# Shifting three layouts of on-chip memory by a few hundred bytes

## The chip, the cores and the metric

The kernel runs on one NeuronCore of a Trainium2 chip, as one program. The metric is the device time of one execution in microseconds. TensorE (PE in the profile) does the matrix products out of SBUF, the on-chip memory of 128 partitions, into PSUM; VectorE (DVE), ScalarE (ACT) and GpSimd (POOL) do the element-wise work; DMA queues bring the weights in.

## The reference

One decoder layer on 512 tokens of width 1024, in float32:

```python
h = h + 0.5 * swiglu(rmsnorm(h, ffn1_norm), ffn1_w_gate, ffn1_w_up, ffn1_w_down)   # width 2816
proj = rmsnorm(h, mix_norm) @ w_in                     # 1024 -> u, v, z, xbc, dt
ya = rmsnorm(chunked_spatial_gating(gelu(u), gelu(v), ...), gm_out_norm)
yb = mamba2_mixer(z, xbc, dt, ...)                     # chunked state-space scan
h = h + concat([ya, yb]) @ w_out
h = h + 0.5 * swiglu(rmsnorm(h, ffn2_norm), ffn2_w_gate, ffn2_w_up, ffn2_w_down)
gate = sigmoid(rmsnorm(h, ple_norm) @ ple_w_gate + ple_b_gate)
h = h + gate * (p @ ple_w_proj)
return rmsnorm(h, final_norm)
```

## The kernel before

**Products.** Each float32 operand is split into a rounded part and a remainder (`hi` and `lo`, type float32r), and each product of 128x128 weights with a tile of activations is three matmuls: hi·hi, hi·lo, lo·hi (`passes`). In a matmul one operand is loaded into the array first (a weight load, 128 columns, 512 bytes of each partition), and the other streams through it (256 or 512 columns, 1024 or 2048 bytes of each partition). The weight load of the next matmul runs while the present one streams. The two feed-forward networks use a Strassen-like scheme with seven products, on half the tokens each, so their matmuls have 256 columns (tiles `xfa` and `xfb` stream against `whi` and `wlo`); their first group of columns is done in the plain way with 512 columns.

**Order.** All operations are recorded once, and then issued in a fixed list of steps (`ORDER`). The change leaves this list as it is. Semaphores are worked out from which instruction touches which bytes.

**Memory.** SBUF is laid out in three parts. The base part (`sb`: `tmp`, `h`, `raw`, `whi`, `wlo` and small tiles) stays for the whole kernel and ends at byte 90,976 of each partition. Above it stands a left layout, and down from byte 229,344 a right layout; both are exchanged as the kernel goes on: `ffn1_left`, `mix_left`, `ffn2_left`, `ple_left`, and `ffn1_right`, `mix_right`, `ffn2_right`, `ple_right`. `REGION` (line 55) says which tile is on which side. When a layout is opened (`open_now`, line 342) or closed (`close_now`, line 350), `pad` (line 331) adds an empty tile of `PAD[...]` bytes (line 61). On the left it stands in front of the tiles and moves them up; on the right it stands above them and moves them down. A new layout's tile waits for the users of the old tiles whose bytes it takes.

All large tiles of one layout have sizes that are multiples of 1024 bytes (2060 for `convin` apart), so all of them begin at the same remainder by 512. The weights within a tile are read in pieces of 512 bytes, so a tile's remainder is that of every piece. The remainders by 512, with `whi` and `wlo` of the base part at 384:

| tiles, layout | first byte before | remainder | first byte after | remainder |
|---|---|---|---|---|
| `whi`, `wlo` (base) | 54,144 and 66,432 | 384 | the same | 384 |
| `xfa`, `xfb` (ffn left) | 91,072 and 107,456 | 448 | 91,456 and 107,840 | 320 |
| `x` (mix left, ple left) | 91,136 | 0 | 91,520 | 384 |
| `ghi`, `glo`, `whix`, `wlox` (ffn right) | 163,808 to 225,248 | 480 | 163,712 to 225,152 | 384 |
| `ya`, `yb` (mix right) | 163,712 and 196,480 | 384 | the same | 384 |

What streams against what, and the distance of the streamed operand's first byte from that of the weights being loaded, by 512:

| streamed, loaded | where | distance before | after |
|---|---|---|---|
| `xfa`/`xfb`, `whi`/`wlo` | up and gate products of both networks | 64 | 448 (that is -64) |
| `x`, `whi`/`wlo` | input projections, final gate | 128 | 0 |
| `whi`/`wlo`, `x` | projection of v | 384 | 0 |
| `ghi`/`glo`, `whix`/`wlox` | down products | 0 | 0 |
| `ghi`/`glo`, `whi`/`wlo` | the other down products, per-layer embedding | 96 | 0 |
| `ya`/`yb`, `whi`/`wlo` | output projection | 0 | 0 |

The printed names in the profile are in the order out<-streamed,loaded. Since a recorder issues every operation, all of them have one line, 1943, and groups are told apart by tiles.

Of the kernel before, what the change touches and what calls it, by code (L numbers as in the profile page):

```python
# [57 lines left out]

PAD = {"sb": 0, "ffn_left": 96, "mix_left": 160, "ple_left": 160, "ffn_right": 0, "mix_right": 96, "ple_right": 0}
HEADS = 16
HD = 64
GROUPS = 2
# [218 lines left out]
def layer_kernel(ctx: ExitStack, tc: tile.TileContext, a: dict, out: bass.AP):  # L283
# [47 lines left out]
    def pad(pool, name):  # L331
        n = PAD[name.replace("1", "").replace("2", "")]
        if n:
            pool.tile([P, n // 4], F32, tag="pad", name=name_of("pad"))
# [1717 lines left out]
```

## Time and profile before

| | |
|---|---|
| three runs before | 1113.59, 1114.28 (median), 1115.97 us |
| the profiled execution's own time | 1115.11 us |
| its span from the first to the last instruction | 1113.4 us |
| mean granted TensorE clock | 0.993 |
| busy: PE, weight loads, DVE, ACT, POOL | 1099.0, 967.6, 765.0, 520.2, 127.5 us |

The span is 1.7 us shorter than the execution's time; the rest lies around the instructions. A matmul's recorded duration is longer than its turn, because the next one begins to stream before it has drained: the turn of a matmul is read as the time from its start to the next one's start in the timeline, which merges neighbours of one kind into one row (x2 means two).

### The profile page before, as it was taken

What the parts mean: (1) busy time and instruction counts of PE and PEld (TensorE: products, weight loads), DVE (VectorE), ACT (ScalarE), POOL (GpSimd) and SP (SyncE); (2) the same over time, 40 slices, a digit from 0 to 9 for tenths busy, and PEclk for the clock granted to TensorE, in tenths of its full rate; (3) what the DMA queues carried; (4) which work ended last, traced back from release to release, by engine and by line L of the source; (5) the groups of instructions that cost most, each with busy time, mean ns of one, the idle gap of its engine ahead of it and who ended that gap; (6) DMA issues with size and microseconds to landing.
All of it is one profiled execution on the core that took longest, in us unless ns stands there. A gap on an engine that the chain in (4) does not pass through costs nothing.

```text
span 1113.4 us, 16384 instructions
## 1 busy us (share of the span) xinstructions
PE 1099.0 (99%) x6631; PEld 967.6 (87%) x6631; DVE 765.0 (69%) x1072; ACT 520.2 (47%) x715; POOL 127.5 (11%) x124
## 2 busy tenths in 40 slices
PE   8999999999999999999999999999999999999996
PEld 6899999999998777778877878899999999999886
DVE  6977666666667468766649876687765666766656
ACT  7544443434435336866424444455434433434445
POOL 1100010000000200123103000101100000000212
PEclk9999999999999999999999999999999999999997
DMA  9788468564631224542314133767837674643412
GB/s 318 207 213 245 109 202 229 146 190 133 152 95 57 82 90 153 160 136 79 114 62 133 38 106 122 208 184 179 217 93 204 169 204 139 166 103 123 133 38 76
DMA packets 49036, 161.66 MB, mean 145 GB/s; under 512 B 5568, under 2 KB 5824, under 8 KB 48960
## 3 DMA queue, kind: packets, MB, share of 16 engines
q1 hardware_dynamic: 34128, 117.46, 31.3%
q0 software_dynamic: 9232, 33.56, 16.3%
q10 hardware_dynamic: 5600, 9.60, 2.9%
q8 instruction: 52, 0.85, 0.3%
q14 instruction: 24, 0.20, 0.1%
HBM read 156.33 MB, written 4.26 MB: 144 GB/s over the span
## 4 chain that ended last, share of the span: by engine, by line
PE 92%; DVE 5%; DMA 1%; ACT 1%; issue 1%; POOL 0%; ACTq 0%; SPq 0%; POOLq 0%
PE b L1943 92%; DVE tmp L1943 1%; DVE wlo L1943 1%; DVE xs L1943 1%; DMA g<-in_p 1%; DVE u L1943 0%; DVE x L1943 0%; DVE h L1943 0%; POOL ssum L1943 0%; DVE ya L1943 0%; DMA cs_dram<-csrow 0%; DVE yb L1943 0%; ACT tmp L1943 0%; DVE convin L1943 0%; ACT whi L1943 0%
## 5 line engine op out<-in xcount | busy, mean ns | idle before, releaser
L1943 PE MATMUL b<-xfb,whi 128*128 128x256 f32 (+1 forms) x1664 | 305.8, 284 | 0.0
L1943 PEld LDWEIGHTS b<-xfb,whi 128*128 128x128 f32 x1664 | 259.2, 188 | 7.0 <-issue 1.0
L1943 PE MATMUL b<-xfb,wlo 128*128 128x256 f32 (+1 forms) x832 | 236.3, 284 | 0.0
L1943 DVE TENSOR_TENSOR wlo<-raw,whi 128x1024 fp32r<-128x1024 f32 (+1 forms) x139 | 173.8, 1254 | 66.3 <-ACT whi L1943 66.3
L1943 ACT CAST whi<-raw 128x1024 fp32r<-128x1024 f32 (+1 forms) x140 | 145.1, 1040 | 147.5 <-PE b L1943 107.4
L1943 PE MATMUL b<-x,whi 128*128 128x512 f32 (+1 forms) x640 | 189.3, 382 | 0.7 <-ACT x L1943 0.4
L1943 PEld LDWEIGHTS b<-xfb,wlo 128*128 128x128 f32 x832 | 156.2, 188 | 1.4
L1943 PEld LDWEIGHTS b<-x,whi 128*128 128x128 f32 x640 | 116.1, 188 | 26.5 <-issue 1.5
L1943 PE MATMUL b<-xfa,whi 128*128 128x256 f32 (+1 forms) x704 | 134.4, 289 | 0.0
L1943 PE MATMUL b<-x,wlo 128*128 128x512 f32 (+1 forms) x312 | 117.9, 378 | 0.3 <-DVE wlo L1943 0.3
L1943 PE MATMUL b<-ghi,whix 128*128 128x512 f32 x296 | 116.6, 394 | 0.0
L1943 PE MATMUL b<-ghi,wlox 128*128 128x512 f32 x296 | 116.5, 394 | 0.0
L1943 PE MATMUL b<-glo,whix 128*128 128x512 f32 x296 | 115.3, 390 | 0.0
L1943 PEld LDWEIGHTS b<-xfa,whi 128*128 128x128 f32 x704 | 110.8, 188 | 3.9
L1943 PE MATMUL b<-xfa,wlo 128*128 128x256 f32 (+1 forms) x352 | 102.0, 290 | 0.0
L1943 ACT CAST whi<-rawb 128x1024 fp32r<-128x1024 f32 x52 | 54.5, 1048 | 79.7 <-PE b L1943 56.0
L1943 DVE TENSOR_TENSOR wlo<-rawb,whi 128x1024 fp32r<-128x1024 f32 x52 | 63.3, 1221 | 40.8 <-ACT whi L1943 40.7
L1943 DVE SCALAR_TENSOR_TENSOR h<-b,h 128x512 f32<-128x512 f32 x96 | 64.3, 685 | 29.3 <-PE b L1943 28.9
L1943 ACT CAST whix<-rawd 128x1024 fp32r<-128x1024 f32 (+1 forms) x40 | 39.4, 986 | 84.1 <-PE b L1943 73.2
L1943 PEld LDWEIGHTS b<-x,wlo 128*128 128x128 f32 x312 | 58.7, 188 | 12.6 <-DVE wlo L1943 1.0
L1943 PEld LDWEIGHTS b<-xfa,wlo 128*128 128x128 f32 x352 | 66.1, 188 | 1.4
L1943 DVE TENSOR_TENSOR wlox<-rawd,whix 128x1024 fp32r<-128x1024 f32 (+1 forms) x40 | 45.6, 1140 | 31.1 <-ACT whix L1943 31.1
(229 smaller groups left out, 1644.0 us busy)
## 6 DMA issues: line engine op xcount, KB each, us to landing
raw<-in_ffn_gu SPq DMA_DIRECT2D x56, 512.0 KB, 5.6
rawd<-in_ffn_down SPq DMA_DIRECT2D x40, 512.0 KB, 4.5
rawb<-in_ffn_gu SPq DMA_DIRECT2D x32, 512.0 KB, 5.7
raw<-in_ffn_gu POOLq DMA_DIRECT2D x30, 512.0 KB, 7.6
raw<-in_w_in SPq DMA_DIRECT2D x29, 512.0 KB, 3.7
s<-in_ffn_gu SPq DMA_DIRECT2D x20, 512.0 KB, 5.5
s<-in_ffn_gu POOLq DMA_DIRECT2D x20, 512.0 KB, 7.7
raw<-in_w_out SPq DMA_DIRECT2D x16, 512.0 KB, 3.7
```

What stands on the lines that cost most here:

```text
L1943: getattr(getattr(real, engine), what)(*(real_of(x) for x in args), **{k: real_of(x) for k, x in kw.items()})
```

## The change

The padding of every left layout grows by 384 bytes. On the right, the two layouts that had no padding get 96 bytes, which the mixing layout has already. Nothing else is changed: the operations, their engines, their order and their shapes are the same.

```diff
-PAD = {"sb": 0, "ffn_left": 96, "mix_left": 160, "ple_left": 160, "ffn_right": 0, "mix_right": 96, "ple_right": 0}
+PAD = {"sb": 0, "ffn_left": 480, "mix_left": 544, "ple_left": 544, "ffn_right": 96, "mix_right": 96, "ple_right": 96}
```

All layouts still fit: the highest left tile ends at byte 159,104 (`mix_left`), and the lowest right tile begins at 159,552 (`mix_right`).

## The prediction

> **What bounds the kernel now.** I read the page's busy times first, then the chain of work that ended last, then TensorE's waits, then the timeline of TensorE in stretches without interruption.
>
> ```profile
> span 1113.4 us, 16384 instructions
> PE 1099.0 (99%) x6631; PEld 967.6 (87%) x6631; DVE 765.0 (69%) x1072; ACT 520.2 (47%) x715; POOL 127.5 (11%) x124
> PE 92%; DVE 5%; DMA 1%; ACT 1%; issue 1%; POOL 0%; ACTq 0%; SPq 0%; POOLq 0%
> ...
> PE b L1943 <- DVE tmp L1943: 3.2, 3, 1.7
> ...
> PE b L1943 <- DVE ya L1943: 0.3, 1, 0.3
> PE b L1943 <- DVE x L1943: 0.3, 1, 0.3
> ```
>
> PE is busy 99% of the span, the chain is PE for 92%, and the longest wait of PE on another engine adds up to 3.2 us. The time is therefore the sum of the matmuls' turns. The change alters no instruction, so it can act in two ways: through the turn of a matmul, if that depends on where its operands lie, or through waits, since it shifts which old bytes a new tile takes.
>
> Whether a turn depends on addresses is asked of the timeline. In each pair below, the first and last row are matmuls of the same kind in a stretch of threes (hi·hi, hi·lo, lo·hi); the first column is the start. First `x` against `whi`/`wlo` (distance 128 by 512), then `yb` against them (distance 0):
>
> ```profile
> 405.62 0.40 PE L1943 MATMUL b<-x,wlo 128*128 128x512 f32 x1
> 405.85 0.63 PE L1943 MATMUL b<-x,whi 128*128 128x512 f32 x2
> ...
> 409.12 0.39 PE L1943 MATMUL b<-x,wlo 128*128 128x512 f32 x1
> ...
> 626.97 0.39 PE L1943 MATMUL b<-yb,wlo 128*128 128x512 f32 x1
> 627.20 0.62 PE L1943 MATMUL b<-yb,whi 128*128 128x512 f32 x2
> ...
> 629.69 0.39 PE L1943 MATMUL b<-yb,wlo 128*128 128x512 f32 x1
> ```
>
> Five threes of `x` take 3.50 us, 233.3 ns a matmul; four of `yb` take 2.72 us, 226.7 ns. Shape, weight tiles and granted clock are the same:
>
> ```profile
> 405.50:412.50 7.00, 7.00 (x32) 5.63 (x31) 6.83 (x12) 2.63 (x4) 0.00 (x0) 1.00 0.27 75
> 626.00:633.00 7.00, 7.00 (x32) 5.79 (x32) 4.63 (x7) 5.16 (x8) 0.00 (x0) 1.00 0.26 75
> ```
>
> Columns: PE, PEld, DVE, ACT, POOL, clock, DMA share, GB/s. The clock is 1.00 and DMA alike in both; DVE is busier in one, ACT in the other. What differs is where the streamed tile lies. Further distances:
>
> ```profile
> 346.66 0.39 PE L1943 MATMUL b<-ghi,wlo 128*128 128x512 f32 x1
> ...
> 348.76 0.39 PE L1943 MATMUL b<-ghi,wlo 128*128 128x512 f32 x1
> ...
> 907.47 0.40 PE L1943 MATMUL b<-ghi,whix 128*128 128x512 f32 x1
> ...
> 909.55 0.39 PE L1943 MATMUL b<-ghi,whix 128*128 128x512 f32 x1
> ...
> 910.92 0.39 PE L1943 MATMUL b<-ghi,whix 128*128 128x512 f32 x1
> ...
> 14.52 0.40 PE L1943 MATMUL b<-xfa,wlo 128*128 128x512 f32 x1
> ...
> 16.59 0.39 PE L1943 MATMUL b<-xfa,wlo 128*128 128x512 f32 x1
> ```
>
> Distance 96 (`ghi` on `whi`): nine matmuls in 2.10 us, 233.3 ns. Distance 0 with both operands at remainder 480 (`ghi` on `whix`): nine in 2.08 us, 231.1 ns, then six in 1.37 us, 228.3 ns: such a stretch starts slower and settles towards 227. Distance 64 (`xfa` in the plain steps, 512 columns): nine in 2.07 us, 230.0 ns. So the order by distance is 0 (227), 64 (230), 96 and 128 (233). `whix` and `whi` lie in different layouts and at different remainders, and yet distance 0 tends to 227 in both: the distance between the two operands read at once decides, as if the weight load, which runs in the stream's shadow, held the stream up more or less.
>
> The 256-column matmuls are the greater part. Here are `xfb`/`xfa` on `whi`/`wlo` (distance 64) and the final gate's `x` in halves (distance 128):
>
> ```profile
> 899.93 0.28 PE L1943 MATMUL b<-xfb,wlo 128*128 128x256 f32 x1
> ...
> 903.11 0.28 PE L1943 MATMUL b<-xfa,wlo 128*128 128x256 f32 x1
> ...
> 1078.30 0.28 PE L1943 MATMUL b<-x,wlo 128*128 128x256 f32 x1
> ...
> 1080.78 0.28 PE L1943 MATMUL b<-x,wlo 128*128 128x256 f32 x1
> ```
>
> 27 matmuls in 3.18 us are 117.8 ns each; 21 in 2.48 us are 118.1 ns.
>
> **The change part by part.** Counts and mean recorded durations, which move with the turns (395 against 389 in the two clean stretches would be the same step as 233.3 against 226.7):
>
> ```profile
> L1943 PE MATMUL b<-x,whi 128*128 128x512 f32 x544 | 172.1, 399 | 0.7 <-ACT x L1943 0.4 <-DVE x L1943 0.3
> L1943 PE MATMUL b<-x,wlo 128*128 128x512 f32 x264 | 104.4, 395 | 0.3 <-DVE wlo L1943 0.3
> L1943 PE MATMUL b<-whi,x 128*128 128x512 f32 x128 | 42.7, 401 | 0.0
> L1943 PE MATMUL b<-wlo,x 128*128 128x512 f32 x64 | 25.3, 396 | 0.7 <-DVE wlo L1943 0.7
> L1943 PE MATMUL b<-ya,wlo 128*128 128x512 f32 x64 | 25.0, 390 | 0.0
> L1943 PE MATMUL b<-xfb,whi 128*128 128x256 f32 x1600 | 285.9, 279 | 0.0
> L1943 PE MATMUL b<-xfa,wlo 128*128 128x256 f32 x320 | 89.5, 280 | 0.0
> L1943 PE MATMUL b<-x,whi 128*128 128x256 f32 x96 | 17.1, 281 | 0.0
> ```
>
> *Left, `x` moves to remainder 384* (input projections, projection of v, final gate). 544 + 264 + 128 + 64 = 1000 matmuls of 512 columns come to the distance of `ya` and `yb`. The `wlo` rows compare best, being freer of the long first matmuls after a pause: 395 with `x`, 390 with `ya`, over all their steps and settling times. 5 ns x 1000 = -5.0 us. Ends: 0 if distance isn't the cause, -6.6 us if all settle at once (1000 x 6.6 ns). I take -5.0. The 96 + 48 halves of the final gate (144 matmuls) go the same way: -0.2 us at 1 ns each.
>
> *Right, down products on `whi` and `wlo`*: `ghi` and `glo` come from distance 96 to 0. Three kinds of 72 matmuls, 216; between 233.3 and 231.1 (unsettled) or 226.7 (settled) lie 2.2 to 6.6 ns, so 0.5 to 1.4 us; I take 4 ns, -0.9 us.
>
> *Right, down products on `whix` and `wlox`*: 888 matmuls move, but both operands by the same 96 bytes. Distance 0 stays 0, and since remainders 480 and 384 settle alike, 0. If 480 itself cost something, the stretch at 228.3 would be 226.7, at most -1.4 us.
>
> *Left, `xfa` and `xfb`*: 1600 + 800 + 640 + 320 = 3360 matmuls of 256 columns, and 192 of 512, go from distance 64 to -64. No row shows -64; it is the unknown of this change. Against symmetry and for it there is one hint: `whi` streaming on `x` lies at 384, which is -128, and its `wlo` row (396) is within 1 ns of `x` at +128 (395). The bounds: if a weight load could disturb a 256-column stream as much as a 512-column one, the whole swing of 6.6 ns would lie open, and from 64, about half way up (230.0), that is 3.3 ns either way: 3360 x 3.3 = 11.1 us less or more. But the 256-column rows at 64 and 128 differ by 0.3 ns, where the 512-column rows differ by 3.3, so they react far less. I take 0, as nearest to those rows, and keep -11.1 and +11.1 for the range.
>
> *Waits.* On the left, old and new tiles keep their offset, all having moved by 384. On the right the networks' tiles now begin on the same bytes as pairs of `ya` and `yb` (163,712), where they straddled by 96 bytes: a new tile waits for one old tile where it waited for one or two. Waits can go and none is added. PE's waits for `ya` (0.3 us) and `x` (0.3) bound the gain; I take 0. DMA destinations move too:
>
> ```profile
> raw<-in_ffn_gu SPq DMA_DIRECT2D x56, 512.0 KB, 5.6
> rawb<-in_ffn_gu SPq DMA_DIRECT2D x32, 512.0 KB, 5.7
> ```
>
> `raw` at remainder 384 lands in 5.6 us and `rawb` at 480 in 5.7, so DMA gains or loses nothing that matters. Where PE runs faster, DVE and ACT have less time to deliver; in the mixing stages they have slack (6.83 of 7.00 us DVE in the first stretch is the tightest), and I add 0.3 us for it.
>
> The sum: -5.0 - 0.2 - 0.9 + 0 + 0 + 0.3 = -5.8 us against the profiled execution (1115.1 to 1109.3). The median of the runs lies 0.8 us lower, at 1114.3, so 1108.5 us.
>
> **A rule that speaks against it.** The Trainium skill's page "SBUF — State Buffer", section "Who interferes with whom", gives TensorE two independent read ports, one for the streamed operand and one for weight loads, and says "PE and ACT never wait on anyone." By it no address would matter and the time would stay at 1114.3. The trace speaks against it: 233.3 and 226.7 ns for the same matmul. The page "TensorE: Matmul & The Clock Gate", section "Wait — 56ns, not 53.3ns?", gives columns / 2.4 GHz + 2.5 ns for back-to-back matmuls, which would be an estimate of 215.8 and 109.2 ns; the trace's 226.7 and 117.8 are above both.
>
> **The rivals.**
> 1. *-64 helps the networks too.* The 3360 turns of 117.8 fall by 1 to 3.3 ns: -3.4 to -11 us on top, 1097.5 to 1105. For it: 64 isn't the best distance for 512 columns (230.0 against 226.7), and the optimum need not be at 0. Against: 256-column rows hardly react.
> 2. *-64 hurts the networks.* Slower than before decides itself at (5.8 + 2.2) / 3360 = 2.4 ns a matmul, turns of 120.2; at the whole 3.3 ns the time is 1108.5 + 11.1 = 1119.6. For it: nothing in the trace shows -64, and 96 and 128 are worse than 64. Against: the same small reaction; and the equal rows at -128 and +128.
> 3. *The addresses don't matter* (what differs between `x` and `yb` is their stage or side of the memory, not the distance): 1114.3. For it: `x` always lies left and `yb` right. Against: `ghi` on `whi` lies right and is slow too (233.3).
>
> **How the numbers follow.** About 0.2% (2.2 us) is what a measurement of this kernel can tell from no change. Forecast, mixing gains and networks unchanged within 3 us: 0.50, 1105 to 1111.5. Rival 1: 0.20. Rival 2: 0.17, of which 0.03 still end faster, 0.06 within 0.2%, 0.08 slower. Rival 3: 0.13, of which 0.11 same and 0.02 slower by something unseen. Faster 0.73, same 0.17, slower 0.10. The range runs from 1099 (most of rival 1) to 1116 (rival 3 and the milder half of rival 2), leaving out about 0.05 below and 0.09 above.
>
> **What would show it.** `x` on `wlo` in the mixing stage: 226.7 ns in settled threes and a mean of 390, where it was 395. `ghi` on `wlo`: below 231. `ghi` on `whix`: as before. `xfb` on `wlo`: 117.8 within 1 ns; each 1 ns off is 3.4 us. PE's waits as before, 3.2 us the longest sum. The prediction is wrong if `x` keeps 233.3, or if the 256-column turn moves by more than 2 ns.

## The result and the profile after

The changed kernel takes 1106.22 us (median; 1105.54 to 1107.15), beside 1113.93 (1112.53 to 1115.97) for the kernel before: a ratio of 0.993, 95% interval 0.9912 to 0.9947. The profiled execution took 1107.15 us, 8.0 us less than the one before (1115.11).

The page of the kernel after, its span and busy times:

```profile
span 1105.4 us, 16386 instructions
PE 1091.1 (99%) x6631; PEld 966.8 (87%) x6631; DVE 764.9 (69%) x1072; ACT 520.4 (47%) x715; POOL 127.2 (12%) x124
```

PE's busy time falls by 7.9 us (from 1099.0) and the span by 8.0; every other engine is where it was. So the gain lies inside the matmuls' turns, as the prediction had placed it. PE's waits after (sum in us, count, longest in us):

```profile
PE b L1943 <- DVE tmp L1943: 3.2, 3, 1.7
PE b L1943 <- DVE wlo L1943: 1.6, 2, 1.2
...
PE b L1943 <- ACT x L1943: 0.7, 1, 0.7
...
PE b L1943 <- ACT ghi L1943: 0.3, 1, 0.3
```

The groups of matmuls by tiles and shape (busy us, mean ns of one), first two of before that the prediction did not show:

```profile
L1943 PE MATMUL b<-ghi,wlox 128*128 128x512 f32 x296 | 116.5, 394 | 0.0
L1943 PE MATMUL b<-ghi,wlo 128*128 128x512 f32 x72 | 28.2, 392 | 0.0
```

and then after:

```profile
L1943 PE MATMUL b<-xfb,whi 128*128 128x256 f32 x1600 | 285.8, 281 | 0.0
L1943 PE MATMUL b<-x,whi 128*128 128x512 f32 x544 | 169.4, 394 | 1.0 <-ACT x L1943 0.7 <-DVE x L1943 0.3
L1943 PE MATMUL b<-ghi,wlox 128*128 128x512 f32 x296 | 115.1, 389 | 0.0
L1943 PE MATMUL b<-x,wlo 128*128 128x512 f32 x264 | 103.2, 391 | 0.4 <-DVE wlo L1943 0.4
L1943 PE MATMUL b<-ghi,wlo 128*128 128x512 f32 x72 | 28.7, 399 | 0.0
```

`x` on `whi` and `wlo` is 5 and 4 ns shorter (399 and 395 before). `ghi` on `wlox`, of the kind that the prediction left at zero, is 5 ns shorter too. `xfb`, the largest group, has not moved (285.9 before). Only `ghi` on `wlo` seems to go the wrong way, 392 to 399; the timeline below says why.

Turns are read from the timeline of TensorE after, each pair of rows the first and the last of an unbroken stretch of threes:

```profile
401.74 0.39 PE L1943 MATMUL b<-x,wlo 128*128 128x512 f32 x1
...
410.58 0.39 PE L1943 MATMUL b<-x,wlo 128*128 128x512 f32 x1
...
183.69 0.28 PE L1943 MATMUL b<-xfb,wlo 128*128 128x256 f32 x1
...
194.29 0.28 PE L1943 MATMUL b<-xfb,wlo 128*128 128x256 f32 x1
194.41 0.39 PE L1943 MATMUL b<-ghi,whix 128*128 128x512 f32 x1
...
198.49 0.39 PE L1943 MATMUL b<-ghi,whix 128*128 128x512 f32 x1
...
1070.12 0.28 PE L1943 MATMUL b<-x,wlo 128*128 128x256 f32 x1
...
1077.68 0.28 PE L1943 MATMUL b<-x,wlo 128*128 128x256 f32 x1
```

`x`: 39 matmuls in 8.84 us, 226.7 ns (233.3 before). `xfb`/`xfa`: 90 in 10.60 us, 117.8, as before. `ghi` and `glo` on `whix`: 18 in 4.08 us, 226.7 from the first matmul on. The final gate's halves: 63 in 7.56 us, 120.0, a little slower than the 118.1 before. And the start of the kernel:

```profile
7.87 0.63 PE L1943 MATMUL b<-ghi,wlo 128*128 128x512 f32 x1
...
10.43 0.63 PE L1943 MATMUL b<-ghi,wlo 128*128 128x512 f32 x1
```

Six matmuls in 2.56 us, 426.7 ns each: in this execution TensorE was still slow here, and came to about 231 ns only after 11 us. Three `ghi`,`wlo` rows at 630 (7.87, 9.15 and 10.43) instead of 390 raise the mean over 72 by 240 x 3 / 72 = 10 ns, which is more than the 7 ns by which it rose. (The Trainium skill's page "TensorE: Matmul & The Clock Gate", section "Wait — 56ns, not 53.3ns?", gives 426.7 ns for 512 columns while the array is cold; this trace agrees in the number.) The granted clock fits this: its first record, at full speed, begins 11.03 us into this span and 4.88 us into the span before, where in both the turns of 427 ns end. In the trace of the left side alone, the first experiment below, the clock is on record as 0.5 from 9.72 to 13.13 us, and the turns from 9.86 to 12.85 us are 427 ns.

Adding up all turns by kind, each from a matmul's start to the next one's, with the waits that fall into them, gives the account (us):

| kind | matmuls | before | after | difference |
|---|---|---|---|---|
| `x` with `whi`/`wlo`, either way, 512 columns | 1000 | 239.1 | 235.6 | -3.5 |
| `ghi`/`glo` on `whix`/`wlox` | 888 | 204.6 | 201.3 | -3.3 |
| `ghi`/`glo` on `whi`/`wlo` | 216 | 52.0 | 51.4 | -0.6 |
| `xfa`/`xfb`, 256 columns | 3360 | 396.1 | 395.6 | -0.5 |
| `xfa`/`xfb`, 512 columns | 192 | 44.1 | 44.9 | +0.8 |
| `x`, 256 columns | 144 | 17.1 | 17.3 | +0.2 |
| `ya`/`yb` on `whi`/`wlo` | 384 | 89.4 | 89.4 | 0.0 |
| all matmuls | 6631 | 1106.1 | 1098.1 | -8.0 |

The 447 matmuls of other kinds give the missing -1.1 us, nearly all of it at the two ends of the kernel: at the start, and in the last 20 us, where the granted clock falls to 0.5 in both traces (from 1097.1 us on before, from 1093.1 us on after).

### The profile page after: what moved, and what is told of

Read it like the earlier page. It is cut to its first block, busy times and chain, and to the rows that moved or that the text cites. A ratio compares the mean times of both kernels' runs of the same rounds, so it can differ in the third digit from the quotient of the medians.

```text
span 1105.4 us, 16386 instructions
## 1 busy us (share of the span) xinstructions
PE 1091.1 (99%) x6631; PEld 966.8 (87%) x6631; DVE 764.9 (69%) x1072; ACT 520.4 (47%) x715; POOL 127.2 (12%) x124
## 4 chain that ended last, share of the span: by engine, by line
PE 91%; DVE 5%; ACT 1%; DMA 1%; POOL 1%; issue 1%; ACTq 0%; SPq 0%; POOLq 0%; DVEq 0%
PE b L1943 91%; DVE tmp L1943 1%; POOL ssum L1943 1%; DVE wlo L1943 1%; DVE xs L1943 1%; DVE u L1943 0%; DVE x L1943 0%; DVE h L1943 0%; DMA g<-in_p 0%; DVE ya L1943 0%; DMA cs_dram<-csrow 0%; ACT tmp L1943 0%; ACT whi L1943 0%; DVE yb L1943 0%; DVE convin L1943 0%
## 5 line engine op out<-in xcount | busy, mean ns | idle before, releaser
L1943 PE MATMUL b<-x,whi 128*128 128x512 f32 (+1 forms) x640 | 186.8, 378 | 1.0 <-ACT x L1943 0.7
L1943 PEld LDWEIGHTS b<-xfb,wlo 128*128 128x128 f32 x832 | 159.3, 191 | 1.5
```

The costliest lines, as they stand in the source:

```text
L1943: getattr(getattr(real, engine), what)(*(real_of(x) for x in args), **{k: real_of(x) for k, x in kw.items()})
```

## Experiments

### Is it the distance, the place, or something else?

In the expectations D is the prediction's theory, that the distance between the streamed operand and the loaded weights sets the turn, and P that a tile's own place does. The four kernels below were timed together on one chip.

**The left side alone.**

```diff
-PAD = {"ffn_left": 96, "mix_left": 160, "ple_left": 160, "ffn_right": 0, "mix_right": 96, "ple_right": 0, ...}
+PAD = {"ffn_left": 480, "mix_left": 544, "ple_left": 544, "ffn_right": 0, "mix_right": 96, "ple_right": 0, ...}
```

> The change's left padding alone; the right layouts as before. Theory D (the distance of the streamed operand from the weights being loaded, by 512 bytes, sets a matmul's turn): x on whi and wlo comes to distance 0 and takes about 227.4 ns a turn (232.7 before), whi on x about 228, xfa and xfb with 512 columns 233, with 256 columns 117.5; ghi on whi stays at distance 96 and 233. ghi on whix stays at distance 0: 230 if its slow starts come from remainder 480, 227 if they come from the state in which the 256-column stretch ahead leaves the engine. Time 1109.5 us in the first case, 1106.6 in the second. Theory W (the gain is waits that fall away where right tiles line up): nothing gained, 1114 us.

Measured: 1096.76 us, ratio to before 0.9852 (0.9837 to 0.9867). Half of the change is faster than the whole of it, by 9.5 us, which neither theory had foreseen. Its largest group:

```profile
L1943 PE MATMUL b<-xfb,whi 128*128 128x256 f32 x1600 | 276.4, 277 | 0.0
```

And its timeline in the stretch shown above of the whole change, with the same tiles in the same order:

```profile
183.01 0.28 PE L1943 MATMUL b<-xfb,wlo 128*128 128x256 f32 x1
...
193.21 0.28 PE L1943 MATMUL b<-xfb,wlo 128*128 128x256 f32 x1
193.34 0.39 PE L1943 MATMUL b<-ghi,whix 128*128 128x512 f32 x1
...
195.41 0.39 PE L1943 MATMUL b<-ghi,whix 128*128 128x512 f32 x1
```

The 90 matmuls of `xfb`/`xfa` take 10.20 us, 113.3 ns, where the whole change has 117.8, with `xfa`, `xfb`, `whi` and `wlo` on the very same bytes in both kernels. By the account, the 3360 turns sum to 382.9 us (396.1 before, 395.6 with the whole change). The undisturbed turns of `x` have a mean of 227.6 ns, as in the whole change (227.4; 232.7 before). `ghi` on `whix` starts slowly, as before: nine in 2.07 us by the rounded rows, 2.08 us in the trace's nanoseconds, 231.1 ns each; from about the eleventh on it takes 226.7.

**The right side alone.**

```diff
-PAD = {"ffn_left": 96, "mix_left": 160, "ple_left": 160, "ffn_right": 0, "mix_right": 96, "ple_right": 0, ...}
+PAD = {"ffn_left": 96, "mix_left": 160, "ple_left": 160, "ffn_right": 96, "mix_right": 96, "ple_right": 96, ...}
```

> The change's right padding alone; the left layouts as before. Theory D: ghi and glo on whi come to distance 0, 227 ns where it was 233 (216 matmuls, -1.3 us); x stays at 232.7 and xfa/xfb at 117.7. ghi on whix: 227 if remainder 480 was the cause of its slow starts (-3 us more), 230 if the stretch ahead is. Time 1112.7 or 1109.7 us. Theory W: the whole gain, 1106 us, with all turns as before.

Measured: 1111.87 us, ratio 0.9983 (0.9971 to 0.9994). Its timeline:

```profile
345.53 0.39 PE L1943 MATMUL b<-ghi,wlo 128*128 128x512 f32 x1
...
347.57 0.39 PE L1943 MATMUL b<-ghi,wlo 128*128 128x512 f32 x1
```

`ghi` on `wlo` comes to 226.7 ns (nine in 2.04 us), the undisturbed turns of `x` keep their mean of 232.7, and the mean of `ghi` on `wlox` falls from 394 to 391 ns, 3 of the 5 ns that it falls by in the whole change; by the account all products on `whix` and `wlox` gain 1.5 us of 3.3. So the two halves do not add: by the medians they gain 16.8 and 1.7 us apart, and 7.7 us together.

**Everything moved by the same 64 bytes by 512.** The base part grows by a small tile, left pads stay, and the right pads grow by 448, and so move the right tiles down by 448, which is up by 64 by 512: every distance is that of before, and no tile is at its old remainder.

```diff
+    constant("shift", (P, 16))
-PAD = {..., "ffn_right": 0, "mix_right": 96, "ple_right": 0}
+PAD = {..., "ffn_right": 448, "mix_right": 544, "ple_right": 448}
```

> Every large tile, weights included, moves by 64 by 512: base tiles up by 64 bytes, left tiles with them, right tiles down by 448. All distances are those of before, all remainders are others (x 64, whi 448, ghi and whix 32, xfa 0). Theory D: every turn as before (x 232.7, ghi on whi 233, ghi on whix 230, xfb 117.7, yb 227.5 ns), time 1114 us. Theory P (the place of the streamed tile alone sets the turn): x, ghi and xfb have new places and their turns change by some ns; the time leaves 1114 by several us in one direction or the other.

Measured: 1114.09 us, ratio 1.0004 (0.9993 to 1.0016). Its groups (the lines of the code are one further):

```profile
L1944 PE MATMUL b<-xfb,whi 128*128 128x256 f32 x1600 | 285.9, 280 | 0.0
L1944 PE MATMUL b<-x,wlo 128*128 128x512 f32 x264 | 104.4, 395 | 0.3 <-DVE wlo L1944 0.3
```

Both are those of before, to 0.1 us. A place that all tiles change together, by these 64 bytes, does nothing.

**The weights moved, the streamed tiles left at their remainders.** The base part grows by 128 bytes, which moves `whi` and `wlo`; the left pads are 384 larger, so that `x`, `xfa` and `xfb` stand at the remainders they had. Distances to `whi` become those of the change (0 and -64), and `ya` and `yb`, which do not move, come from 0 to -128.

```diff
+    constant("shift", (P, 32))
-PAD = {"ffn_left": 96, "mix_left": 160, "ple_left": 160, ...}
+PAD = {"ffn_left": 480, "mix_left": 544, "ple_left": 544, ...}
```

> Base tiles (whi and wlo among them) move up by 128; left and right tiles keep the remainders of before (x 0, xfa 448, ghi and whix 480, ya and yb 384). Theory D: x on whi is now at distance 0, 227.4 ns, with x where it was by 512; xfa and xfb at -64 (256 columns 117.5 ns, 512 columns 233.3); ya and yb on whi, which have not moved, come to distance -128 and get slower, 232.7 instead of 227.5 ns. ghi on whi comes to -32: not known, 227 to 231. Time about 1111 us (-5.2 for x, +2.0 for ya and yb, +0.4 for xfa and xfb), or 3 less if ghi on whix settles at once. Theory P: all as before, 1114 us.

Measured: 1110.49 us, ratio 0.997 (0.9962 to 0.9979). Its groups, then its timeline:

```profile
L1944 PE MATMUL b<-x,wlo 128*128 128x512 f32 x264 | 103.2, 391 | 0.4 <-DVE wlo L1944 0.4
L1944 PE MATMUL b<-ya,wlo 128*128 128x512 f32 x64 | 25.3, 395 | 0.0
```

```profile
622.21 0.39 PE L1944 MATMUL b<-yb,wlo 128*128 128x512 f32 x1
...
631.97 0.39 PE L1944 MATMUL b<-yb,wlo 128*128 128x512 f32 x1
```

`x` becomes fast without a change of its remainder, and `ya` and `yb` slow without a change of theirs: 42 matmuls in 9.76 us, 232.4 ns (226.7 before). With the kernel before it this settles D against P for these matmuls: the distance decides, and the weights are one end of it.

`ghi` on `whix`, of which neither end was moved against the other, starts slowly here:

```profile
194.94 0.39 PE L1944 MATMUL b<-ghi,whix 128*128 128x512 f32 x1
...
197.02 0.39 PE L1944 MATMUL b<-ghi,whix 128*128 128x512 f32 x1
```

Nine in 2.08 us, 231.1 ns, where the whole change has 226.7 from the first on. The stretch of `xfb` ahead is the same in both by distance (-64) and by turn (117.8 ns).

### Which distances, and with what period?

From here to the last but one, each kernel was timed in one execution only, and nine executions of the kernel before spread from 1112.1 to 1116.1 us; so what is read from these seven is the turns. `pad` is changed so that the first and the second network can have pads of their own, and what is not named stays as in the whole change.

```diff
-        n = PAD[name.replace("1", "").replace("2", "")]
+        n = PAD.get(name, PAD.get(name.replace("1", "").replace("2", ""), 0))
```

**`xfa`/`xfb` at -32 and -96, `x` at 256, halves at 64.**

```diff
+PAD = {..., "ffn1_left": 512, "ffn2_left": 448, "mix_left": 800, "ple_left": 96}
```

> The changed kernel, but with another left padding in each layout: xfa and xfb of the first network at distance -32 from whi, of the second at -96, x of the mixing stage at 256, x of the final gate at 64. Theory D512 (the pattern repeats after 512 bytes): x at 256 has a turn of its own, not 227.4. Theory D256 (it repeats after 256): x at 256 is as at 0, 227.4 ns. 256-column turns: by symmetry of the 512-column rows (64: 229, 96 and 128: 233, -64: 233) -32 should be quicker to settle than -96; 113.3 for -32 and 117.8 for -96 if the lower of the two rhythms found at -64 needs a small negative distance, 117.8 in both if the rhythm is set by what the stretch is entered from (theory S), since the down products are as in the changed kernel.

Measured: 1110.63 us beside 1114.82 before. `x` at distance 256 runs like `x` at 0, by its group:

```profile
L1943 PE MATMUL b<-x,wlo 128*128 128x512 f32 x264 | 103.3, 391 | 0.4 <-DVE wlo L1943 0.4
```

So, as far as this pair shows it, the pattern repeats after 256 bytes. The turns of `xfa`/`xfb` have means of 118.3 ns at -32 and 118.6 at -96, and 113.3, expected as one possibility at -32, does not occur. The final gate's halves, at 64, take 113.4 ns.

**`xfa`/`xfb` at 0 and 128, `x` at -64, halves at -32.**

```diff
+PAD = {..., "ffn1_left": 544, "ffn2_left": 672, "mix_left": 480, "ple_left": 512}
```

> The changed kernel with xfa and xfb at distance 0 in the first network and 128 in the second, x of the mixing stage at -64 and of the final gate at -32. From the final gate's halves (120.0 ns at distance 0, 118.7 at 128): xfb 120.0 in the first network and 118.7 in the second, so the time is 3.8 us (1680 x 2.25 ns) and 1.6 us (1680 x 0.95) worse in them. x with 512 columns at -64: 233, as xfa and xfb in the plain steps; at -32: between 227 and 233.

Measured: 1120.93 us beside 1114.82, the slowest of all. Its timeline in the second network:

```profile
901.45 0.28 PE L1943 MATMUL b<-xfb,wlo 128*128 128x256 f32 x1
...
906.85 0.28 PE L1943 MATMUL b<-xfb,wlo 128*128 128x256 f32 x1
```

`xfb` at 128: 45 matmuls in 5.40 us, 120.0 ns, where 118.7 was expected from the halves of `x`; at 0 the mean of the first network is 119.9. `x` at -64 has a mean of 233.3 ns, although `xfa` at +64 had 230. In the projection of v the same tiles change sides, `whi` and `wlo` streaming and `x` loaded, and so stand at +64: their undisturbed turns have a mean of 229.7. So the sign counts. And 0, the best distance for 512 columns, is with 128 the worst for 256.

### Why do the same 256-column matmuls take 113.3 or 117.8 ns?

The traces of the left side alone and of the whole change hold both numbers: in the whole change too, the first long stretch runs in the lower rhythm, and almost all later ones in the upper. From its timeline:

```profile
61.43 0.28 PE L1943 MATMUL b<-xfa,wlo 128*128 128x256 f32 x1
...
63.13 0.28 PE L1943 MATMUL b<-xfa,wlo 128*128 128x256 f32 x1
```

15 matmuls in 1.70 us, 113.3. The trace of before has the lower rhythm as well, in a single stretch of 24 matmuls at distance 64:

```profile
754.95 0.28 PE L1943 MATMUL b<-xfb,wlo 128*128 128x256 f32 x1
...
757.33 0.28 PE L1943 MATMUL b<-xfb,wlo 128*128 128x256 f32 x1
```

21 turns in 2.38 us, 113.3. In these traces a stretch of 24 to 120 matmuls keeps its rhythm once it has settled; with the exception shown at the end, it changes only where a stretch of 512 columns lies between. There are two theories, S and C in the expectations: S, that the stream has two steady rhythms, and the one in which a stretch enters is the one it keeps; C, that what else goes on in SBUF, writes of the right tiles at their new place above all, disturbs the stream. For the networks, only right pads are changed in the next three kernels, so that `xfa`/`xfb` and their weights stay on the same bytes.

**Down products at distance 64 in the first network, 32 in the second.**

```diff
+PAD = {..., "ffn1_right": 32, "ffn2_right": 64}
```

> The left side as in the changed kernel (xfa, xfb at -64); the right tiles of the first network at distance 64 from whi, of the second at 32 (0 in the changed kernel, 96 with the left padding alone). ghi on whix stays at distance 0. Theory S (the 256-column stretch at -64 has two rhythms, 113.3 and 117.8 ns, and keeps the one that it is entered with; a jump of distance at the entry throws it into the lower): 113.3 where the jump is large enough, as at 96; 117.8 where it isn't. One of 64 and 32 may fall on each side. Theory C (ghi, glo, whix and wlox at remainder 384 disturb the 256-column stream while they are written): 113.3 in both, since none is at 384.

Measured: 1101.55 us beside 1114.82. One execution, both rhythms:

```profile
183.78 0.28 PE L1943 MATMUL b<-xfb,wlo 128*128 128x256 f32 x1
...
189.78 0.28 PE L1943 MATMUL b<-xfb,wlo 128*128 128x256 f32 x1
...
887.07 0.28 PE L1943 MATMUL b<-xfb,wlo 128*128 128x256 f32 x1
...
897.61 0.28 PE L1943 MATMUL b<-xfb,wlo 128*128 128x256 f32 x1
```

First network: 51 matmuls in 6.00 us, 117.6 ns. Second: 93 in 10.54 us, 113.3. The first network's right tiles are away from 384 here and its rhythm is still the upper one, against C; that it depends on what runs in between, with the streams themselves untouched, is what S says.

**Distances -32 and -64.**

```diff
+PAD = {..., "ffn1_right": 128, "ffn2_right": 160}
```

> The left side as in the changed kernel; the right tiles of the first network at distance -32 from whi, of the second at -64, which is the distance of xfa and xfb themselves. Theory S: entry from ghi on whi at -32 and -64; no rhythm is excluded, but within a network nearly all stretches have the same one, and the 512-column stretches start slow (230 ns on average) wherever the entry from xfb on whix isn't at a distance of -64. Theory C: 113.3 in both networks.

Measured: 1109.3 us beside 1114.82; means 117.0 and 117.5, the upper rhythm in all but four stretches of the first network and one of the second, all of them early.

**Distances 128 and -96, and the final gate's halves at 64.**

```diff
+PAD = {..., "ffn1_right": 480, "ffn2_right": 192, "ple_left": 96}
```

> xfa and xfb at -64 as in the changed kernel; right tiles at distance 128 from whi in the first network and at -96 in the second; x of the final gate at 64. Theory S (two rhythms at one distance, kept from entry): each network has 113.3 or 117.8 nearly throughout; so far 96 and 32 gave the lower, 64, 0, -32 and -64 the higher, so for 128 and -96 the chance is about even. A theory in which the left padding alone sets the rhythm is already excluded; one in which every jump over some size gives the lower predicts 113.3 in both (128 and -96 are the largest jumps). ghi on whix: 227 to 230 ns. Final gate: halves 113.3 or 117.7 ns where they were 120.0, -0.3 to -1.0 us.

Measured: 1106.44 us beside 1112.91; means 117.5 and 114.4, the halves at 113.4. In the second network nearly every stretch begins with five turns of 118 to 123 ns and then runs at 113.3. So a rhythm need not be there from the first matmul, and S holds only for a stretch that has settled.

So far 96 (left side alone), 32 and, nearly, -96 lead into the lower rhythm, and 0, 64, -32, -64 and 128 do not. The next two ask whether that holds for `xfa`/`xfb` at +64, the distance of before.

**Left as before, down products at 32 and -32.**

```diff
+PAD = {..., "ffn_left": 96, "ple_left": 96, "ffn1_right": 64, "ffn2_right": 128}
```

> xfa and xfb back at distance 64, as before the change; right tiles at 32 in the first network and -32 in the second; x of the mixing stage at 0 and of the final gate at 64. If 64 is as two-rhythmed as -64 (the final gate's halves at 64 took 113.3 ns, xfa and xfb before the change 117.7), one of the two networks may run at 113.3 ns; if the stream of xfa and xfb at 64 knows only 117.7, both are at 117.7. xfa and xfb with 512 columns: 229 ns (233 at -64).

Measured: 1102.6 us beside 1112.91:

```profile
184.04 0.28 PE L1943 MATMUL b<-xfa,wlo 128*128 128x256 f32 x1
...
190.84 0.28 PE L1943 MATMUL b<-xfb,wlo 128*128 128x256 f32 x1
```

60 matmuls in 6.80 us, 113.3, in the first network; the mean of the second is 117.8. So the distance of before can run nearly throughout in the lower rhythm; the kernel before was in the upper one for all but one stretch.

**Left as before, down products at 64 and -96.**

```diff
+PAD = {..., "ffn_left": 96, "ple_left": 96, "ffn1_right": 32, "ffn2_right": 192}
```

> xfa and xfb at distance 64; right tiles at 64 in the first network (no jump between the streamed operands of the two kinds of stretch) and at -96 in the second; x of the mixing stage at 0 and of the final gate at 64. Theory S: again each network keeps one of the two rhythms, 113.3 or 117.8 ns, nearly throughout. With 32 on the right the lower came at 64 on the left, with 96, 0 and -32 the higher. If the lower needs a jump, 64 on the right gives 117.8 and -96 gives 113.3; a rule for the sign is not known. ghi on whi at 64: 230 ns; at -96: 234.

Measured: 1106.87 us beside 1115.59; means 117.5 and 117.8. The -96 that led to the lower rhythm from a stream at -64 does not from +64, and 96 does not either (the kernel before). A rule by the down products' distance alone is wrong: which entry leads to which rhythm depends on both distances, and these runs do not give the law of it.

### The best version

The left side of the change, the right of before for the networks, and for the last part the pads that gave the fast halves.

```diff
+PAD = {"ffn_left": 480, "mix_left": 544, "ple_left": 96, "ffn_right": 0, "mix_right": 96, "ple_right": 96, ...}
```

> The left padding of the change for the networks and the mixing stage, none on the right for the networks (as before the change), and x of the final gate at distance 64. Theory S: xfa and xfb keep the lower rhythm, 113.4 ns, in both networks, as with the left padding alone; the final gate's halves take 113.3 or 117.8 ns (120.0 there), its 512-column matmuls 229 (227.8): 0 to 0.8 us less than the left padding alone, 1096 to 1097 us; ghi on whix 229.4 and ghi on whi 233 ns as there.

Measured: 1096.96 us (1096.74 to 1097.97), ratio 0.9847 (0.9834 to 0.986). It beats the kernel before by 1.5% and the whole change by about 9 us, and cannot be told from the left side alone (0.9852). The halves came out in the upper rhythm, 117.8, so the part that it was to add is missing.

Its timeline shows both rhythms in one stretch of `xfb` on the same tiles at the same distance:

```profile
770.89 0.28 PE L1943 MATMUL b<-xfb,wlo 128*128 128x256 f32 x1
...
771.61 1.22 DVE L1943 TENSOR_TENSOR wlo<-raw,whi 128x1024 fp32r<-128x1024 f32 x1
...
772.59 0.28 PE L1943 MATMUL b<-xfb,wlo 128*128 128x256 f32 x1
...
772.89 0.19 PEld L1943 LDWEIGHTS b<-xfb,wlo 128*128 128x128 f32 x1
772.93 0.34 PE L1943 MATMUL b<-xfb,wlo 128*128 128x256 f32 x1
...
773.34 0.28 PE L1943 MATMUL b<-xfb,wlo 128*128 128x256 f32 x1
...
775.46 0.28 PE L1943 MATMUL b<-xfb,wlo 128*128 128x256 f32 x1
```

Up to 772.59, 15 matmuls in 1.70 us, 113.3 ns. Then the weight load at 772.89 comes late: DVE finishes a `wlo` at 772.83, and one turn is some 67 ns longer (180 ns by the records). From 773.34 on, 18 matmuls take 2.12 us, 117.8. After a pause of less than a turn the stream was in the other rhythm, and it stayed there to the end of the stretch. This fits S, without a stretch of other matmuls between. The left side alone and the kernel with 128 and -96 have the same break at the same step (turns of 182 and 181 ns). But the kernel with 64 and 32 has the late load too, with a turn of 185 ns from 777.49 us on, and is back in the lower rhythm after three more turns:

```profile
778.26 0.28 PE L1943 MATMUL b<-xfb,wlo 128*128 128x256 f32 x1
...
779.62 0.28 PE L1943 MATMUL b<-xfb,wlo 128*128 128x256 f32 x1
```

12 matmuls in 1.36 us, 113.3. So a late weight load can change the rhythm and need not.

## Why the prediction was right or wrong

The forecast of 1108.5 us was 2.3 us from the measured 1106.22, and faster, as forecast. That it came so close is in part luck, since two errors of opposite sign stand in the sum. Step by step:

- **What bounds it, and that distance acts: right.** PE's busy time took the whole gain. Rival 3, that addresses do not matter, falls with the kernel that moved only the weights. With it falls, for these matmuls, the rule of the Trainium skill's page "SBUF — State Buffer", section "Who interferes with whom", that TensorE never waits on anyone, as a forecast of the time: `yb` on `wlo` takes 226.7 or 232.4 ns, by where the weights lie.
- **`x`, -5.0 us: right in the turn, short in the sum.** The stretch went from 233.3 to 226.7 ns, the mean on `wlo` from 395 to 391. The account shows -3.5 us. Taken turn by turn, 992 of the 1000 became 5.07 ns shorter on average, -5.0 us, and the other eight 1.5 us longer together, with the waits that fall into them: PE's waits for `wlo` grew from 1.0 to 1.6 and for `x` from ACT from 0.4 to 0.7, and the weight load that follows the last `x` on `wlo` of the mixing stage now waits 0.57 us for DVE's `ya` instead of 0.19. PE was faster and DVE was not. The slack term of 0.3 us was the mis-sized one.
- **`ghi` on `whi`, -0.9 us: right.** It runs at 226.7 ns. The account has -0.6, with the slow start of this execution in it.
- **`ghi` on `whix`, 0: wrong, and the largest error, -3.3 us.** Distance 0 did stay 0 and the settled turn stayed 226.7, but the slow start of each stretch is gone. The step that failed is the inference from "both operands by the same 96 bytes" to no gain: it took the distance within the stretch for all that counts. Over the 48 stretches of at least 12 that follow `xfa`/`xfb`, the first nine turns have a mean of 231.8 ns before, 231.2 with the left side alone, 230.7 with the right side alone, 231.7 with the weights moved, and 226.7 with the whole change; from the thirteenth on the longer stretches are at 226.7 in all five. So neither side alone brings the fast start; the distance within the stretch, 0 in all five, does not explain it; and nor does the rhythm of the stretch ahead, which is the upper one before, with the right side alone and with the weights moved. What sets it stays open. The lower bound of -1.4 us was too narrow, since it looked at one nearly settled stretch instead of counting the unsettled ones.
- **`xfa`/`xfb`, 256 columns, 0: right in number, not in reason.** Measured -0.5 us. The reasoning was that such matmuls hardly react to the distance. They react with 113.3 to 120.0 ns, 3360 x 6.7 = 22.5 us, and the stream was in the upper of two rhythms, at 64 before and at -64 after. The row that would have shown it was in the trace of before, 24 matmuls at 113.3 ns between thousands at 117.8, and I had read one stretch and not asked for the spread. Rival 1 priced -64 at -3.4 to -11 us; with the left side alone it was -13.2.
- **Symmetry of + and -: wrong.** `x` streaming at -64 has 233.3 ns, and `whi` and `wlo` streaming on `x` at +64 have 229.7 in the same trace; `xfa` on 512 columns went from 64 to -64 and lost 0.8 us.
- **The final gate's halves, -0.2 us: wrong sign.** At distance 0 they take 120.0 ns, +0.2 us. What is best for 512 columns was carried over to 256 without a row.
- **Waits and DMA, 0: near enough.** PE's waits for `ya` and for `x` from DVE stay at 0.3; for ACT's `ghi` it went from 1.4 to 0.3, at the start, where the matmuls of 426.7 ns stand instead.

The terms in short: `x` gave 1.5 us less than forecast, `ghi` on `whix` 3.3 more, and the small ones nearly cancel.

## What to carry to other kernels

Where TensorE is the bound and each matmul loads its weights in the shadow of the one before, as with the float32r matmuls here (no other type was run), the addresses of the streamed tile and of the weights are a tuning parameter: compare their distance by 256 bytes, read the turn from start to start over unbroken stretches of the timeline, and price each shape by itself. Test halves of a change alone, since here one half was worth 16.8 us and both together 7.7. Where a trace shows two values of the turn for the same tiles, even in one stretch of many, ask what ran ahead of it before pricing the shape at the commoner value.

## What the runs showed of the hardware

- The turn depends on the distance of the streamed operand from the weights, and a shift of all tiles by 64 bytes changes nothing. At 256 it is as at 0 (`x` streaming has 227.4 ns at both), and at -128 (232.4) nearly as at 128 (232.7), which fits a period of 256 bytes. For 512 columns the means of undisturbed turns are about 227 ns at 0, 229 at 64, 233 at 32, 96, 128, -32 and -64, and 234 at -96; for 256 columns 118 to 120 at 0, 128, -32 and -96, and 113.3 or 117.8 at 64 and at -64.
- The lowest turns are 226.7 and 113.3, which is its half. That the weight load and the stream collide in SBUF is my reading of it; no run shows the collision itself. In an unbroken stretch the weights being loaded and the weights in use have the same remainder, so the turns do not tell which of the two counts.
- At 64 and -64 the 256-column stream has two rhythms, 4.5 ns apart. A stretch settles into one within about five turns and then keeps it, unless a weight load comes late. In a kernel of 3360 such matmuls this is worth up to 3360 x 4.5 = 15 us. A weight load late by some 70 ns changed it in three kernels and did not in a fourth. Which entry gives which is open.
